# The weight pipeline of a two-layer hybrid trunk: low parts asked for three pieces ahead, later coefficients, a split eviction of u

## The chip, the cores and the metric

The kernel runs on one core of a Trainium2 chip. The core has a matrix engine (PE, with PEld for its weight loads), a vector engine (DVE), a scalar engine (ACT), GpSimd (POOL), a sync engine (SP) that here only starts DMAs, and 16 DMA engines. Each engine works off its own instructions in the order in which they were written and waits on semaphores for the others. The metric is the device time of one execution in microseconds (us); less is better.

## The reference, cut to what matters

Input x is 256 tokens of 2048 features in fp32. There are two layers; each is a mixer and a feed-forward block:

```python
h = rmsnorm(x);  z = h @ W_in            # z = [q | k | v | u | gate_attn | gate_ssm]
A = sliding_window_attention(q, k, v)     # 16 heads of 64, 4 kv heads, window 128, ALiBi, sinks
s_t = a * s_(t-1) + B u_t                 # 64 groups, 64 complex states each, over all positions
B = glu(gelu(Re(C s) + D u))
m = sigmoid(gate_attn) * (A @ W_ab) + sigmoid(gate_ssm) * (B @ W_sb)
x = x + m @ W_out
x = x + (silu(h2 @ W_gate) * (h2 @ W_up)) @ W_fo     # h2 = rmsnorm(x), inner width 5632
```

All of it is compared in fp32.

## The kernel before

**Pieces.** Activations are kept transposed, features on the partitions and 256 tokens along the free axis, each value as a high and a low part. All weights come as 881 pieces of 128 x 4 x 256 fp32 (512 KB, one DMA each from SP, line 91). ACT casts the high part of a piece, `whi` (L106), DVE subtracts it from the piece and so makes the low part, `wlo` (L121), and PE multiplies (L295): 8 matmuls of 128x512 with `whi` (against both parts of the activation), then 8 of 128x256 with `wlo`. (In the very first slab of layer 0 they go one by one, at L303.) The pools hold four raw pieces (`LOADS`), four `whi` and four `wlo` (`PARTS`).

**Lead.** `Weights.get(i)` stands ahead of the matmuls of piece i: it writes the instruction for the high part of piece i+3, for the low part of piece i+2, and the load of piece i+6. `low` itself begins with `self.high(upto, cuts)`, so a low part that is asked for brings its high part with it if that is not written yet.

**Ticks.** `Clock` orders everything else. After the matmuls of each piece `products` calls `ck.tick()`, which writes the jobs that are due: `later(n, f)` is a call n ticks on, `stages(n, gen)` runs a generator a `yield` at a time, one tick apart, `at(n, ...)` counts from the start of the layer. So each engine's queue is: the instructions of `get(i)`, the matmuls of piece i (PE only), the jobs of the tick, then `get(i+1)`.

**A layer.** Slabs of W_in go first: u (4 slabs of 4 pieces), k and v, q (4 slabs), then the gates of the attention branch (`ga`), W_ab in 8 slabs of 2 pieces, and the gates of the state-space branch (`gs`). After these come W_glu, W_sb, W_out and the feed-forward block. Into the ticks of these slabs are put:

- the state-space scan (L757 to L769): 127 steps, each of two multiplications (L766) and four additions (L769) on DVE, spread evenly from tick `s0 = v0 + 9` to tick 110. `states_in` (PE and ACT) fills the state `S` at the eight ticks from `v0`. After the last step PE computes `ys` (L963) from `S`.
- `attend(j)`, 8 times a layer: scores on PE and a maximum on DVE (L855); a tick later the exponentials on ACT (L862), the denominator and its reciprocal on DVE (L864, L865), and four scalings on ACT with that reciprocal (L869); two ticks later the transposes, then the product with v and the split of the result into `ya` (ACT L351, DVE L161).
- the evictions of the `gs` slabs: a copy (ACT L343), an addition and a multiplication by the norm (DVE L344, L943), and two sigmoids (ACT L363).
- in layer 0 alone, ahead of the scan, the coefficients of both layers' state spaces, some 600 short DVE instructions from tick 1 (`coefficients`, `prepare`, L1115 to L1118).

**The start.** The first norm has its squares on ACT (L404), their sums on GpSimd (L412), and a matmul `ms` with a matrix of ones (L417) at tick 5, which needs the sums. Lines 429 to 437 write the first pieces' high and low parts around them: low parts of pieces 0 to 2 ahead of the squares, the high part of piece 3 after two squares and that of piece 4 after six. `evict_u` (L716 to L731) scales a slab of u on DVE and, in the same job, copies it into the layout of the states, four copies on ACT and four on DVE.

Of the kernel before, what the change touches and what calls it, by code (L numbers as in the profile page):

```python
# [49 lines left out]
class Weights:  # L50
# [76 lines left out]
            self.n_low += 1  # L127

    def get(self, i):
        self.high(i + 3)  # L130
        self.low(i + 2)
        self.load(i + 2 + self.LOADS)
        return self.ready.pop(i)


class Clock:
# [6 lines left out]
    def later(self, n, fn, *args):  # L143
        self.jobs.setdefault(self.now + max(n, 1), []).append((fn, args))

    def stages(self, n, gen, step=1):


        def go():
            if next(gen, "end") != "end":  # L150
                self.later(step, go)

        if n > 0:
            self.later(n, go)
        else:
            go()
# [11 lines left out]
def build(ctx, tc, a, out):  # L168
# [18 lines left out]
    def p8(x, shape, dt=F32):  # L187
        return big.tile(shape, dt, name=nm(x), tag="p8", bufs=8)
# [11 lines left out]
    later, stages = ck.later, ck.stages  # L200


    W = Weights(nc, wp)
# [136 lines left out]
    def whole(ps, x="wh"):  # L340

        t = t2(x)
        s.copy(t, ps[:, :, T:])  # L343
        v.tensor_add(t, t, ps[:, :, :T])  # L344
        return t
# [79 lines left out]
    def x_in(i):  # L425
        return xs[i // 4][:, 2 * (i % 4) : 2 * (i % 4) + 2, :]
# [3 lines left out]
    for i in range(8):  # L430
        norm.feed(i, x_in(i))
        if i in lows:
            W.low(lows[i])
    for i in range(8):
        if i in (2, 6):
            W.high(3 + i // 4)
        norm.square(i, x_in(i))


# [3 lines left out]
    def vexp(dst, x, w):  # L443
        n, r, q = w
        v.tensor_scalar(dst, x, -103.9, 88.7, ALU.max, ALU.min)
        yield
        v.tensor_scalar(n, dst, math.log2(math.e), MAGIC, ALU.mult, ALU.add)
        yield
        v.tensor_scalar_sub(n, n, MAGIC)
        yield  # L450
        v.scalar_tensor_tensor(r, n, -0.693359375, dst, ALU.mult, ALU.add)
        yield
        v.scalar_tensor_tensor(r, n, 2.12194440e-4, r, ALU.mult, ALU.add)
        yield
        v.tensor_scalar_mul(q, r, 1.9875691500e-4)
        yield
        for c in (1.3981999507e-3, 8.3334519073e-3, 4.1665795894e-2, 1.6666665459e-1, 5.0000001201e-1):
            v.scalar_tensor_tensor(q, q, c, r, ALU.add, ALU.mult)
            yield
        v.scalar_tensor_tensor(q, q, 1.0, r, ALU.add, ALU.mult)  # L460
        yield
        v.tensor_scalar_add(dst, q, 1.0)
        yield

        half = r
        v.tensor_scalar(half, n, 0.5, MAGIC, ALU.mult, ALU.add)
        yield
        v.tensor_scalar_sub(half, half, MAGIC)
        yield
        v.tensor_sub(n, n, half)  # L470
        yield
        for m in (half, n):
            v.tensor_scalar(m, m, 127.0, 8388608.0, ALU.add, ALU.mult)
            yield
            v.tensor_copy(q.bitcast(I32), m)
            yield
            v.tensor_mul(dst, dst, q)
            yield
# [83 lines left out]
    def coefficients():  # L562
        v.tensor_reduce(pmask, ident.rearrange("p (q g h) -> p g q h", g=2, h=16), axis=AX.XY, op=ALU.add)
        v.tensor_scalar_mul(qg, qkg[:, :, 0], 0.125)
        ww = p8("cw", [P, 11, NC])
        w = [ww[:, i, :] for i in range(8)]
        dt, mag, th = (ww[:, i, :] for i in range(8, 11))
        yield from vexp(dt, ldt, w[:3])
        v.tensor_mul(mag, lam_r, dt)
        v.tensor_mul(th, lam_i, dt)  # L570
        chains = [vexp(mag, mag, w[:3]), vsincos(a_i, a_r, th, w[3:8])]
        while chains:
            chains = [c for c in chains if next(c, "end") != "end"]
            yield
        den, p, q, ar1, p2, q2 = w[:6]
        v.tensor_mul(a_r, a_r, mag)
        v.tensor_mul(a_i, a_i, mag)
        v.tensor_mul(den, lam_r, lam_r)
        v.tensor_scalar_sub(ar1, a_r, 1.0)
        v.tensor_mul(p2, lam_i, lam_i)  # L580
        yield
        v.tensor_mul(p, ar1, lam_r)
        v.tensor_mul(q, a_i, lam_i)
        v.tensor_add(den, den, p2)
        v.tensor_mul(p2, a_i, lam_r)
        v.tensor_mul(q2, ar1, lam_i)
        yield
        v.tensor_add(f_r, p, q)
        v.reciprocal(p, den)
        v.tensor_sub(f_i, p2, q2)  # L590
        yield
        v.tensor_mul(f_r, f_r, p)
        v.tensor_mul(f_i, f_i, p)

        v.tensor_mul(p, a_r, a_r)
        v.tensor_mul(q, a_i, a_i)
        v.tensor_mul(q2, a_r, a_i)
        yield
        v.tensor_sub(p, p, q)
        v.tensor_scalar_mul(n_ai, a_i, -1.0)  # L600
        v.tensor_scalar_mul(q2, q2, 2.0)
        for l in range(L):
            f = slice(32 * l, 32 * l + 32)
            yield
            v.tensor_copy(scan_c[:, l, 0, 0, :], p[:, f])
            v.tensor_copy(scan_c[:, l, 1, 1, :], p[:, f])
            v.tensor_copy(scan_c[:, l, 1, 0, :], q2[:, f])
            v.tensor_scalar_mul(scan_c[:, l, 0, 1, :], q2[:, f], -1.0)

    def sliced(gen, counts):  # L610

        counts = iter(counts)
        n = next(counts)
        for _ in gen:
            n -= 1
            while n <= 0:
                yield
                n = next(counts, 5)
# [86 lines left out]
    def layer(l, norm):  # L705
# [4 lines left out]
        def at(n, fn, *args):  # L710
            later(t0 + n - ck.now, fn, *args)
# [5 lines left out]
        def evict_u(i, ps, wide):  # L717
            x = whole(ps) if wide else ps[:, :, :T]
            v.tensor_mul(
                u[:, 2 * i : 2 * i + 2, :, :].rearrange("p s m c -> p s c m"),  # L720
                x.rearrange("p s (c m) -> p s c m", m=2),
                over(rms).rearrange("p s (c m) -> p s c m", m=2),
            )
            for j in range(4):
                for m in range(2):
                    o = 64 * (j % 2) + 32 * m
                    dst, src = ur[o : o + 32, 4 * i + j // 2 : 4 * i + 4 : 2, :], u[32 * j : 32 * j + 32, 2 * i : 2 * i + 2, m, :]
                    if m:
                        v.tensor_copy(dst, src)
                    else:  # L730
                        s.copy(dst, src)  # L731
# [19 lines left out]
        for i in range(4):  # L751
            wide = l > 0 or i > 0
            ps = slab((l, "in", 6 + i), norm.rhs, wide)
            later(1 if i else 3, evict_u, i, ps, wide)
        v0 = 17 if l else 30
        for n in range(8):
            at(v0 + n, states_in, n)  # L757

# [13 lines left out]
        def c_times_a():  # L772
            hold["cc"] = cw = p8("cc", [P, 4, 32, 16])
            for i, n in enumerate(("c_re", "c_im")):
                nc.sync.dma_start(cw[:, i], a[n][:, l])
            yield
            v.tensor_scalar_mul(cw[:, 1], cw[:, 1], -1.0)
            for i, signs in ((0, (a_r, a_i)), (1, (n_ai, a_r))):
                yield
                w = t2("ct", [P, 32, 16])  # L780
                v.tensor_mul(cw[:, 2 + i], cw[:, 0], per_pair(signs[0], l))
                v.tensor_mul(w, cw[:, 1], per_pair(signs[1], l))
                yield
                v.tensor_add(cw[:, 2 + i], cw[:, 2 + i], w)

        at(10 if l else 24, stages, 0, c_times_a())


        s0, s1 = v0 + 9, 110
# [31 lines left out]
        ps = slab((l, "in", 4), norm.rhs, True)  # L821
        stages(1, normed(kt, ps, qkg[:, l, 1:2]))
        ps = slab((l, "in", 5), norm.rhs, True)
        stages(1, values(ps))
        for i in range(4):
            ps = slab((l, "in", i), norm.rhs, True)
# [71 lines left out]
        for i in range(8):  # L898
            if i % 4 == 0:
                ga.append(p8("ga", [P, 8, T]))  # L900
            ps = slab((l, "in", 10 + i), norm.rhs, True)
# [16 lines left out]
        for i in range(8):  # L918
            ps = slab((l, "ab", i), lambda k: ya[k // 4][:, k % 4, :, :], True)
# [76 lines left out]
        for i in range(8):  # L996
            if i % 4 == 0:
                gs.append(p8("gs", [P, 8, T]))
            ps = slab((l, "in", 18 + i), norm.rhs, True)
# [14 lines left out]
        for i in range(4):  # L1014
            ps = slab((l, "glu", i), lambda k: yg[:, 0, k, :, :], True)
# [13 lines left out]
        for i in range(2, 8):  # L1029
            ps = slab((l, "sb", i), lambda k: yg[:, 1, k, :, :], True)  # L1030
# [13 lines left out]
        for i in range(8):  # L1044
            xo = t2("xo")
            nc.sync.dma_start(xo, src[:, 2 * i : 2 * i + 2, :])
            ps = slab((l, "o", i), lambda k: mg[:, k, :, :], True)
# [28 lines left out]
        for part, nf in enumerate(FPARTS):  # L1076
            hid = [p8("hid", [P, 4, 2, T], F32R) for _ in range(nf // 4)]
            for i in range(nf // 2):
                ps = slab((l, "fg", f0 // 2 + i), norm2.rhs, True)
                stages(3 if part == 0 and i == 0 else 1, gate(ps, i))  # L1080
                ps = slab((l, "fu", f0 // 2 + i), norm2.rhs, True)
# [14 lines left out]
            for i in range(8):  # L1096
# [3 lines left out]
                ps = slab((l, "fo", part, i), hrhs, True)  # L1100
# [11 lines left out]
            f0 += nf  # L1112
        return nxt

    stages(1, sliced(coefficients(), (5, 5, 5, 5, 4, 4, 4)))  # L1115
    first = prepare(0, v, 1)
    later(1, next, first)
    stages(15, first)  # L1118
    for l in range(L):
        norm = layer(l, norm)  # L1120
    ck.flush()
# [60 lines left out]
```

## Time and profile before

| what | us |
|---|---|
| median of three runs | 2632.5 (2630.88 to 2633.15) |
| the profiled execution | 2632.42 |
| its span, first to last instruction | 2630.5 |
| PE busy in the span | 2591.1 (99%) |
| DVE busy | 1932.4 (73%) |
| ACT busy | 1267.8 (48%) |
| GpSimd busy | 29.0 (1%) |

The profiled execution is within 0.1 us of the median, and 1.9 us of it lie outside the span. The shares are means over stages of different kinds: forty equal slices of the span show DVE at 90% or more in five of them and at 50 to 70% in most others, so each stage is to be read by itself.

### The profile page before, as it was taken

To read this page: it belongs to the slowest core of one execution; us is meant where nothing else is said; L and a number is where in the kernel's file an instruction comes from. 1 tells how busy PE (TensorE), PEld (TensorE's weight loads), DVE (VectorE), ACT (ScalarE), POOL (GpSimd) and SP (SyncE) were. 2 spreads that over 40 slices of the span, in tenths; PEclk is the share of its full clock that TensorE was granted. 3 is DMA by queue.
4 is the path that set the end of the run, shared out by engine and by line. 5 is a ranking of instruction groups with operands and counts; after the bars stand their busy time and mean duration, and the time that the engine had idled before them with its cause. 6 is when DMAs were issued, how large, how long until landed. Compare 5 with 4: busy or idle time off the path is not lost.

```text
span 2630.5 us, 40564 instructions
## 1 busy us (share of the span) xinstructions
PE 2591.1 (99%) x15716; PEld 2259.7 (86%) x15716; DVE 1932.4 (73%) x3648; ACT 1267.8 (48%) x1725; POOL 29.0 (1%) x34
## 2 busy tenths in 40 slices
PE   7999899999999999999999999999999999999999
PEld 6878788888888888888888788888888888888888
DVE  8889997866765666566677999887666656665664
ACT  5666545544443444334455675465544434443442
POOL 2000000000000000000000000000000000000000
PEclk9999999999999999999999999999999999999999
DMA  6544455666655565566664445556656556655655
GB/s 203 169 129 144 145 170 164 200 209 194 203 172 191 190 189 179 192 199 187 199 201 160 141 149 170 178 173 211 213 185 187 183 199 188 190 186 187 188 180 172
DMA packets 139825, 477.85 MB, mean 182 GB/s; under 512 B 14960, under 2 KB 25456, under 8 KB 139632
## 3 DMA queue, kind: packets, MB, share of 16 engines
q1 hardware_dynamic: 139488, 475.06, 56.4%
q8 instruction: 123, 2.02, 0.3%
q14 instruction: 70, 0.57, 0.1%
q10 hardware_dynamic: 144, 0.20, 0.0%
HBM read 471.01 MB, written 4.19 MB: 181 GB/s over the span
## 4 chain that ended last, share of the span: by engine, by line
PE 81%; DVE 14%; ACT 3%; issue 1%; DMA 0%; SPq 0%; ACTq 0%; DVEq 0%
PE acc L295 79%; DVE wlo L121 5%; DVE S L769 3%; DVE sc L766 2%; ACT whi L106 1%; DVE wh L344 1%; DVE scs L855 1%; PE v L746 1%; PE ys L963 1%; ACT scs L869 1%; DVE ga L896 0%; DVE ga L916 0%; DMA w<-in_w_in 0%; PE acc L323 0%; PE bt L672 0%
## 5 line engine op out<-in xcount | busy, mean ns | idle before, releaser
L106 ACT CAST whi<-w 128x1024 fp32r<-128x1024 f32 (+1 forms) x881 | 910.6, 1047 | 769.6 <-PE acc L295 606.4
L121 DVE TENSOR_TENSOR wlo<-w,whi 128x1024 fp32r<-128x1024 f32 (+1 forms) x881 | 1061.4, 1219 | 221.2 <-ACT whi L106 220.2
L295 PE MATMUL acc<-h,whi 128*128 128x512 f32 x4448 | 1128.6, 396 | 0.8 <-DVE wh L344 0.8
L295 PEld LDWEIGHTS acc<-h,whi 128*128 128x128 f32 x4448 | 802.3, 189 | 156.8 <-issue 9.4
L295 PEld LDWEIGHTS acc<-h,wlo 128*128 128x128 f32 x4448 | 606.1, 190 | 53.5 <-DVE wlo L121 10.9
L295 PE MATMUL acc<-h,wlo 128*128 128x256 f32 x4448 | 621.8, 283 | 5.3 <-DVE wlo L121 5.3
L295 PE MATMUL acc<-hid,whi 128*128 128x512 f32 x1384 | 346.6, 392 | 0.0
L295 PEld LDWEIGHTS acc<-hid,whi 128*128 128x128 f32 x1384 | 248.9, 189 | 44.5
L337 DVE TENSOR_REDUCE j<-acc 128x512 f32<-128x1024 f32 x88 | 107.8, 1225 | 134.4 <-PE acc L295 134.4
L295 PEld LDWEIGHTS acc<-hid,wlo 128*128 128x128 f32 x1384 | 188.8, 190 | 13.5
L295 PE MATMUL acc<-hid,wlo 128*128 128x256 f32 x1384 | 193.0, 282 | 0.0
L1102 DVE TENSOR_TENSOR xn<-xn,acc 128x512 f32<-128x512 f32 x47 | 32.3, 688 | 173.5 <-PE acc L295 173.5
L769 DVE TENSOR_TENSOR S<-S,sc 128x32 f32<-128x32 f32 x1016 | 153.5, 222 | 0.0
L295 PE MATMUL acc<-mg,whi 128*128 128x512 f32 x512 | 128.2, 392 | 0.0
L766 DVE TENSOR_TENSOR sc<-scan_c,S 128x64 f32<-128x64 f32 x508 | 115.6, 269 | 0.0
L295 PEld LDWEIGHTS acc<-mg,whi 128*128 128x128 f32 x512 | 92.1, 189 | 16.5
L295 PE MATMUL acc<-yg,whi 128*128 128x512 f32 x384 | 96.2, 392 | 0.0
L295 PEld LDWEIGHTS acc<-yg,whi 128*128 128x128 f32 x384 | 69.1, 189 | 12.3
L295 PE MATMUL acc<-ya,whi 128*128 128x512 f32 x256 | 68.5, 410 | 10.0 <-DVE ya L161 6.0
L295 PEld LDWEIGHTS acc<-mg,wlo 128*128 128x128 f32 x512 | 69.8, 190 | 5.0
L351 ACT CAST hid<-j 128x512 fp32r<-128x512 f32 x44 | 27.4, 623 | 96.9 <-DVE j L1072 96.9
L295 PE MATMUL acc<-mg,wlo 128*128 128x256 f32 x512 | 71.4, 282 | 0.0
(238 smaller groups left out, 1500.7 us busy)
## 6 DMA issues: line engine op xcount, KB each, us to landing
w<-in_w_fi SPq DMA_DIRECT2D x352, 512.0 KB, 4.3
w<-in_w_in SPq DMA_DIRECT2D x207, 512.0 KB, 3.7
w<-in_w_fo SPq DMA_DIRECT2D x176, 512.0 KB, 4.4
w<-in_w_out SPq DMA_DIRECT2D x64, 512.0 KB, 4.4
w<-in_w_ab SPq DMA_DIRECT2D x32, 512.0 KB, 3.5
w<-in_w_sb SPq DMA_DIRECT2D x32, 512.0 KB, 4.1
w<-in_w_glu SPq DMA_DIRECT2D x16, 512.0 KB, 3.8
x<-in_x SPq DMA_DIRECT2D x8, 256.0 KB, 5.8
```

The source lines that it names most:

```text
L106: self.nc.scalar.copy(part[0][:, f, :], w[:, f, :])
L121: self.nc.vector.tensor_sub(lo[:, f, :], w[:, f, :], hi[:, f, :].bitcast(F32))
L295: pe.matmul(o, w, r, start=start, stop=last and j == m - 1 and lo_part == 1, skip_group_check=True)
L337: v.tensor_reduce(t, ps.rearrange("p s (a t) -> p s t a", a=2), axis=AX.X, op=ALU.add)
L344: v.tensor_add(t, t, ps[:, :, :T])
L351: s.copy(hi, src)
L746: pe.matmul(pss[r][:, c0 : c0 + P], bt[ri][o : o + 64, 2 * q4 + i, :], ur[o : o + 64, 2 * q4 + i, :], start=True, stop=True)
L766: v.tensor_mul(pr, scan_c[:, l, :, :, f], S[:, :, f, c - 1].unsqueeze(1).to_broadcast([P, 2, 2, 16]))
L769: v.tensor_add(S[:, :, f, c], S[:, :, f, c], pr[:, :, r, :])
L855: v.tensor_tensor_reduce(scs[b][:, f, :], scs[b][:, f, :], pv[:, f, :], 1.0, sk[:, b : b + 1], ALU.add, ALU.max, accum_out=mx[:, b, n : n ...
L869: s.activation(z, z, AF.Copy, scale=rd[:, b, n : n + 1])
L1102: v.tensor_add(t, t, ps[:, :, :T])
```

## The change

The change has four parts. (1) `get(i)` now asks for the low part of piece i+3 (which brings the high part of i+3 with it, just ahead) and loads up to piece i+7; the low part of piece 3 is asked for ahead of the first squares, and no high part between them. (2) `evict_u` copies u a tick after it has scaled it. (3) `states_in` of layer 0 begins at tick 34 instead of 30, and with it the scan, whose last tick stays 110; the product `c_times_a` goes from tick 24 to 28. (4) The coefficients begin at tick 5 instead of 1, `prepare` at 19 instead of 15. The pools are as before. After the change the lines from L132 on are one lower, those from 435 on two lower, and those from 724 on one lower again.

```diff
     def get(self, i):
-        self.high(i + 3)
-        self.low(i + 2)
-        self.load(i + 2 + self.LOADS)
+        self.low(i + 3)
+        self.load(i + 3 + self.LOADS)
         return self.ready.pop(i)
...
         if i in lows:
             W.low(lows[i])
+    W.low(3)
     for i in range(8):
-        if i in (2, 6):
-            W.high(3 + i // 4)
         norm.square(i, x_in(i))
...
                 over(rms).rearrange("p s (c m) -> p s c m", m=2),
             )
+            yield
             for j in range(4):
...
-            later(1 if i else 3, evict_u, i, ps, wide)
-        v0 = 17 if l else 30
+            stages(1 if i else 3, evict_u(i, ps, wide))
+        v0 = 17 if l else 34
...
-        at(10 if l else 24, stages, 0, c_times_a())
+        at(10 if l else 28, stages, 0, c_times_a())
...
-    stages(1, sliced(coefficients(), (5, 5, 5, 5, 4, 4, 4)))
+    stages(5, sliced(coefficients(), (5, 5, 5, 5, 4, 4, 4)))
     first = prepare(0, v, 1)
     later(1, next, first)
-    stages(15, first)
+    stages(19, first)
```

What moves in the queues is seen at three places. The first is an `attend` in layer 0. ACT before: the exponentials and scalings of one `attend` (`scs`, `sm`), with the high parts of pieces 56 and 57 (`w_56`, `w_57`) on either side.

```order
L106 CAST whi_2330<-w_56_2186 128x1024
L862 ACTIVATE scs_2303,sm_2301<-scs_2303,sm_2301 128x128
...
L869 ACTIVATE scs_2303<-scs_2303,sm_2301 128x128
L869 ACTIVATE scs_2303<-scs_2303,sm_2301 128x256
L869 ACTIVATE scs_2306<-scs_2306,sm_2301 128x128
L869 ACTIVATE scs_2306<-scs_2306,sm_2301 128x256
L106 CAST whi_2380<-w_57_2224 128x1024
```

DVE before, at the same `attend`: the reciprocal that ACT's L869 needs, the low part of an earlier `ya`, and the next low part of weights, which is that of piece 56.

```order
L864 TENSOR_TENSOR sm_2301<-sm_2301 128x4
L865 RECIPROCAL sm_2301<-sm_2301 128x4
L161 TENSOR_TENSOR ya_1661<-y_2318,ya_1661 128x256
L121 TENSOR_TENSOR wlo_2331<-w_56_2186,whi_2330 128x1024
L766 TENSOR_TENSOR sc_2402<-scan_c,S_1271 128x64
```

ACT's rows stand in the same order after the change. DVE after, at the same place (lines one lower):

```order
L863 TENSOR_TENSOR sm_2256<-sm_2256 128x4
L864 RECIPROCAL sm_2256<-sm_2256 128x4
L160 TENSOR_TENSOR ya_1628<-y_2273,ya_1628 128x256
L121 TENSOR_TENSOR wlo_2336<-w_57_2141,whi_2335 128x1024
L765 TENSOR_TENSOR sc_2357<-scan_c,S_1380 128x64
```

What stands behind the reciprocal on DVE is now the low part of piece 57, whose high part stands on ACT behind the four scalings; before it was that of piece 56, whose high part stands ahead of the exponentials.

The second place is the eviction of a `gs` slab. DVE before, the multiplication by the norm and what follows it:

```order
L344 TENSOR_TENSOR gs_4112<-gs_4112,acc_3912 128x512
L943 TENSOR_TENSOR gs_4112<-gs_4112,rms_126 128x512
L121 TENSOR_TENSOR wlo_4071<-w_95_3959,whi_4070 128x1024
```

DVE after, and ACT after, with the two sigmoids (L362) that need that multiplication:

```order
L343 TENSOR_TENSOR gs_4099<-gs_4099,acc_3899 128x512
L942 TENSOR_TENSOR gs_4099<-gs_4099,rms_126 128x512
L121 TENSOR_TENSOR wlo_4106<-w_96_3946,whi_4105 128x1024
```

```order
L342 COPY gs_4099<-acc_3899 128x512
L362 ACTIVATE gs_3898<-gs_4099,params 128x256 x2
L106 CAST whi_4105<-w_96_3946 128x1024
```

The low part behind the multiplication is now that of piece 96, whose high part stands on ACT behind the sigmoids; before it was piece 95.

The third place is the start. DVE before, from the last parts of h (L400) on; L563 to L453 and L455 are the first coefficients:

```order
L400 SCALAR_TENSOR_TENSOR h_124<-x_78,params,h_124 128x256
L563 TENSOR_REDUCE pmask<-ident 128x2
L564 TENSOR_SCALAR qg<-params 128x2
L445 TENSOR_SCALAR cw_245<-params 128x64
...
L453 SCALAR_TENSOR_TENSOR cw_245<-cw_245 128x64
L121 TENSOR_TENSOR wlo_178<-w_3_93,whi_177 128x1024
L455 TENSOR_SCALAR cw_245<-cw_245 128x64
```

DVE after, from the same place on:

```order
L399 SCALAR_TENSOR_TENSOR h_124<-x_78,params,h_124 128x256
L121 TENSOR_TENSOR wlo_174<-w_3_93,whi_173 128x1024
L121 TENSOR_TENSOR wlo_251<-w_4_211,whi_250 128x1024
L121 TENSOR_TENSOR wlo_281<-w_5_213,whi_280 128x1024
L121 TENSOR_TENSOR wlo_311<-w_6_215,whi_310 128x1024
```

The low parts of pieces 3 to 6 now stand directly behind h, and the coefficients behind them.

## Rows read from the trace of the kernel before

**Rows 1.** The chain that ended last, shares of the span by engine.

```profile
PE 81%; DVE 14%; ACT 3%; issue 1%; DMA 0%; SPq 0%; ACTq 0%; DVEq 0%
```

**Rows 2.** Stretches: window, length, busy us (count) PE, PEld, DVE, ACT, POOL; clock, DMA, GB/s.

```profile
152.00:400.00 248.00, 233.81 (x1375) 195.02 (x1373) 242.85 (x987) 142.06 (x274) 3.63 (x2) 0.98 0.48 152
400.00:1400.00 1000.00, 1000.00 (x6090) 879.70 (x6084) 677.46 (x747) 457.65 (x543) 4.47 (x3) 1.00 0.59 191
1422.00:1694.00 272.00, 266.06 (x1581) 226.76 (x1580) 266.88 (x1011) 161.69 (x298) 3.63 (x2) 0.99 0.52 161
```

**Rows 3.** Timeline: start, duration (us), engine, instruction, [wait before it <-released by]; scan's end, layer 0.

```profile
399.32 3.57 PE L963 MATMUL ys<-S,cb 128*32 128x127 f32 x64 [2.06 <-DVE S L769]
```

**Rows 4.** Timeline, the same in layer 1.

```profile
1693.90 0.60 DVE L769 TENSOR_TENSOR S<-S,sc 128x32 f32<-128x32 f32 x4
1693.97 1.98 PE L963 MATMUL ys<-S,cb 128*32 128x127 f32 x64
```

**Rows 5.** Timeline, an `attend` of layer 0 on DVE and ACT.

```profile
199.81 0.18 DVE L865 RECIPROCAL sm<-sm 128x4 f32<-128x4 f32 x1
199.91 0.39 DVE L161 TENSOR_TENSOR ya<-y,ya 128x256 fp32r<-128x256 f32 x1
200.22 1.22 DVE L121 TENSOR_TENSOR wlo<-w,whi 128x1024 fp32r<-128x1024 f32 x1
200.09 1.50 ACT L869 ACTIVATE scs<-scs,sm 128x128 f32<-128x128 f32 x4 [2.64 <-DVE sm L865]
201.49 1.98 ACT L106 CAST whi<-w 128x1024 fp32r<-128x1024 f32 x2
```

**Rows 6.** Timeline, a low part that waits for its high part before the scan.

```profile
170.66 1.23 DVE L121 TENSOR_TENSOR wlo<-w,whi 128x1024 fp32r<-128x1024 f32 x1 [0.57 <-ACT whi L106]
```

**Rows 7.** Timeline, the eviction of a `gs` slab in layer 0, DVE and ACT.

```profile
351.34 0.69 DVE L943 TENSOR_TENSOR gs<-gs,rms 128x512 f32<-128x512 f32 x1
351.94 1.22 DVE L121 TENSOR_TENSOR wlo<-w,whi 128x1024 fp32r<-128x1024 f32 x1
352.07 0.91 ACT L363 ACTIVATE gs<-gs,params 128x256 f32<-128x256 f32 x2 [2.90 <-DVE gs L943]
352.88 2.93 ACT L106 CAST whi<-w 128x1024 fp32r<-128x1024 f32 x3
```

**Rows 8.** Timeline, the last `ya` of layer 0, DVE and ACT.

```profile
285.36 1.22 DVE L121 TENSOR_TENSOR wlo<-w,whi 128x1024 fp32r<-128x1024 f32 x1
285.44 1.04 ACT L106 CAST whi<-w 128x1024 fp32r<-128x1024 f32 x1 [0.74 <-PE acc L295]
```

**Rows 9.** Timeline, PE in the first 75 us.

```profile
24.81 0.58 PE L303 MATMUL acc<-h,wlo 128*128 128x256 f32 x1 [6.25 <-DVE wlo L121]
33.03 1.02 PE L417 MATMUL ms<-ssq,ones 128*128 128x256 f32 x4
53.71 1.21 PE L295 MATMUL acc<-h,wlo 128*128 128x256 f32 x8 [0.85 <-DVE wlo L121]
67.39 1.22 PE L295 MATMUL acc<-h,wlo 128*128 128x256 f32 x8 [2.25 <-DVE wlo L121]
68.44 3.58 PE L295 MATMUL acc<-h,whi 128*128 128x512 f32 x8
72.81 2.00 PE L295 MATMUL acc<-h,whi 128*128 128x512 f32 x8
```

**Rows 10.** Timeline, DVE and GpSimd at the start.

```profile
23.54 1.21 DVE L121 TENSOR_TENSOR wlo<-w,whi 128x1024 fp32r<-128x1024 f32 x1
16.69 10.56 POOL L412 TENSOR_TENSOR ssq<-ssq,sq 128x512 f32<-128x512 f32 x7 [12.87 <-ACT sq L404]
22.27 3.62 POOL L412 TENSOR_TENSOR ssq<-ssq,sq 128x512 f32<-128x512 f32 x2
```

**Rows 11.** Timeline, the first steps of the scan in layer 0 on DVE.

```profile
154.23 0.46 DVE L766 TENSOR_TENSOR sc<-scan_c,S 128x64 f32<-128x64 f32 x2
155.12 0.47 DVE L766 TENSOR_TENSOR sc<-scan_c,S 128x64 f32<-128x64 f32 x2
168.01 1.20 DVE L121 TENSOR_TENSOR wlo<-w,whi 128x1024 fp32r<-128x1024 f32 x1
```

## The prediction, made before the result was known

> **What bounds the kernel now.** I began with the chain that ended last: PE holds 81% of it and DVE 14% [rows 1]. Only the stages where DVE is on it can answer to a change of DVE's queue, so the second view is the busy time by stretch [rows 2]. From 400 to 1400 us PE is busy in all of 1000 us and DVE in 677: whatever DVE waits for there is covered by 323 us of its own idle time, and I cost the change at nothing there (the last stage is the same block again). The two stretches that hold the scans are different. In layer 0, 152 to 400 us, DVE is busy 242.85 of 248 us, and in layer 1, 1422 to 1694 us, 266.88 of 272. Both end where PE takes the finished state: in layer 0 PE stands 2.06 us waiting for the last scan additions [rows 3], in layer 1 `ys` begins 0.07 us after the last group of additions began [rows 4]. So from the scan's start to its end the time is DVE's work plus DVE's idle time, and there are only some 5 us of that in either. Each microsecond that the change makes DVE stand in these stretches is one of the total. The third view is therefore the timeline of DVE beside ACT, at each place where one waits for the other.
>
> **The change part by part.** *The low part a piece earlier.* Its work is the same: 881 casts and 881 subtractions. What moves is who stands behind whom. Before, the high part that a low part needs was written one `get` earlier; now both are written in the same `get`, so the low part can begin only when ACT has worked off everything up to it, and the matmuls no longer need it for three pieces. Where ACT's queue ahead of that cast itself waits for DVE, DVE stands for a round trip, and its scan steps, queued behind the low part, stand with it.
>
> At an `attend` this is so. DVE finishes the reciprocal at 199.99, ACT starts the four scalings at 200.09, and they take 1.50; the cast behind them starts at 201.49 and one takes 0.99 (two in 1.98), so it ends at 202.48 [rows 5]. DVE now starts its low part at 200.22, behind the low part of `ya`; it would start at 202.48: 2.3 us of standing. A row close to it: behind the first `attend` a low part waits to 170.66 for its high part, 0.57 us, although one scan step now stands ahead of it [rows 6]; the place behind the reciprocal, where it will stand, came at 168.01 [rows 11], 2.65 earlier. So I bound a trip by 0.57 and 2.65 and take the 2.3 of the row in the dense part. It applies to `attend` 0 to 6 (behind the seventh's reciprocal an eviction stands first); in layer 0 the first falls ahead of the later scan. That is 6 + 7 = 13 trips, 13 x 2.3 = 29.9.
>
> At a `gs` eviction the multiplication starts at 351.34, the two sigmoids take 0.91 from 352.07, and three casts start at 352.88, the first of them ending about 353.9 (2.93 for three). The low part now starts at 351.94 [rows 7], and would at 353.9: 2.0 us. Four such evictions lie before the last scan step of each layer: 8 x 2.0 = 16.0.
>
> At the last `ya` the low part at 285.36 would wait for the cast that runs from 285.44 to 286.48 [rows 8]: 1.1 us, in both layers 2.2.
>
> When PE comes to `ys` in layer 1 it will have waited, as in layer 0 now. There the same matmuls take 3.57 after the wait [rows 3] and 1.98 without one [rows 4]: +1.6.
>
> *Loads.* They go up to piece i+7 instead of i+6, each behind the low part that frees its buffer, as before; nothing else stands in SP's queue. DMA engines are busy 0.48 to 0.59 of a stretch [rows 2]: nothing. If a load came late, its cast would, by up to one piece.
>
> *The start.* The low part of piece 3 now stands directly behind h on DVE instead of behind the first coefficients. PE stood 6.25 us for it at 18.56 to 24.81 [rows 9], since DVE came to it at 23.54 [rows 10]. That goes; what is late next is the sum of squares. The seven additions on GpSimd run from 16.69 for 10.56 us; two of them, beside that low part, took 3.62, the other five 6.94, 1.39 each, so one meeting costs 0.84 to 2.23 minus 1.39 = 0.84 us [rows 10]. After the change ACT casts the high part of piece 3 ahead of the squares, so they begin one cast later (1.04, [rows 8]), and four low parts may meet them instead of one: 16.69 + 1.04 + 10.56 + 3 x 0.84 = 30.8, where PE, 6.25 us ahead, is at `ms` (33.03 now) at 26.8 or, at full clock, somewhat earlier. So it waits there again, and comes out 33.03 - 30.8 = 2.2 us ahead. The later waits of 0.85 and 2.25, and the 1.58 us that the next piece takes longer behind the latter (3.58 against 2.00, [rows 9]) go if coefficients that begin four ticks later no longer stand in the way, or come again in other places, since the same instructions are only moved. I bound PE's lead at the scan's start by -3 (all that was gained is lost at `ms`, and the waits come again) and +8 (6.25 + 0.85 + 2.25 + 1.58 = 10.9, less 3 for a shorter wait at `ms`) and take +2, near the `ms` row.
>
> The Trainium skill ("SBUF — State Buffer", section "Who interferes with whom") says that a vector instruction with two inputs in SBUF contends with a GpSimd instruction that reads SBUF, and that the loser waits for the whole instruction. The two slow additions agree; if the four low parts met no addition, the sums would end at 28.3 and the lead be 4.7, the forecast 2.7 lower.
>
> *The later scan.* In layer 0 the scan begins four ticks later with the same last tick. At 168.01, about where it will begin, seven steps lie behind it now, one each 0.89 us (154.23 to 155.12, [rows 11]): 6.2 us of DVE's work are pushed into the full stretch. Given back are one low part, which is by then done ahead (1.22, [rows 5]), and about as much again, my estimate of how much earlier DVE comes to that place without the steps: 6.2 - 2.4 = 3.8, less the lead of 2: +1.8.
>
> *The copies of u* come one tick later, ahead of the scan, and the first `states_in` that needs the last slab stands five ticks behind: nothing; if a copy were late, it would cost up to one piece (2.00 + 1.21 = 3.2, [rows 9]).
>
> The sum: 29.9 + 16.0 + 2.2 + 1.6 + 1.8 = 51.5. The profiled execution took 2632.4, the median of the runs is 2632.5: 2632.4 + 51.5 = **2683.9**, 2.0% slower.
>
> A sentence of the skill bears on the heart of it. The rows show DVE's low part starting as the next thing behind the reciprocal and `ya` [rows 5], with nothing overtaking. The Trainium skill ("TensorE: Matmul & The Clock Gate", the table at its head) gives ScalarE and VectorE strict first-in-first-out queues: by that nothing behind a waiting low part could fill the trip, and the trace agrees (DVE spends the 0.57 of [rows 6] idle, though it has more to do).
>
> **Rivals.** (1) *Faster.* The round trips cost nothing, because DVE comes to them late enough to find the cast done, and the start's waits go: the upper lead of 8, and the 2.06 of [rows 3], since a lead of 8 is more than the 3.8 of the later scan and lets DVE end before PE asks: 10, or **2622**. What decides is whether DVE finds the high part ready behind L865. Against it: the scalings can't begin before that reciprocal, however late DVE is, and stand ahead of the cast. (2) *No change.* The trips are hidden and the start's gain is eaten by `ms` and the denser scan: 2632 to **2634**. (3) *Half.* In layer 1 PE waits little (busy 266.06 of 272, [rows 2]), so its scan may have room that the rows don't show, and only layer 0 counts: 1.8 + 6 x 2.3 + 4 x 2.0 + 1.1 = 24.7, **2657**. Against it are the 0.07 us in rows 4. (4) *The clock too.* Each new wait of PE may be followed by a piece that takes 1.58 longer, as behind the wait of 2.25 [rows 9]. In layer 0 PE has 14 us of room for it, in layer 1, where PE and DVE are equally full, none: 11 trips x 1.58 = 17.4, **2701**.
>
> **How the numbers follow.** The forecast has 0.58, (1) 0.10, (2) 0.07, (3) 0.13, (4) 0.12. A measurement of this kernel tells some 0.2% (5 us) from no change. Faster is (1): 0.10; within it is (2): 0.07; slower are the rest: 0.83. The range leaves out (1) and (2), 0.17. It takes in (3) with 2 us below it and (4) with the upper bound of a trip (13 x 0.35 = 4.6) above it: 2655 to 2706. With trips of only 0.57 the time is 2683.9 - 13 x 1.73 = 2661, and the bounds of the lead move it by -6 and +5, all inside.
>
> **What would show it.** Right: DVE idle in the two scan stretches grows from 5 us to about 25 each, put down to `whi` of ACT on the low part behind each reciprocal and each `gs` multiplication, some 2 us each; PE waits for low parts in about as many places; the last scan addition of layer 0 ends some 25 us later, that of layer 1 some 50. The wait of 6.25 is gone and `ms` starts at 30 to 31. Wrong: low parts behind the reciprocal without a wait; a scan that ends in layer 1 only 25 us later (3); or PE's granted clock falling well below 0.98 in these stretches (4).

## The result and the profile after

The changed kernel takes 2736.97 us (four runs, 2736.5 to 2739.12) against 2632.57 before: 1.0399 times as long, 95% interval 1.0381 to 1.0417, or 104 us more. Slower was forecast, and by the mechanism that was named, but the 51 us forecast are half of it, and the time lies outside the range (2655 to 2706).

The page's chain of the changed kernel, by engine, answers to [rows 1]; under it stands the group of the low parts in the same page (busy us, mean ns, idle before them, what released most of it).

```profile
PE 76%; DVE 16%; ACT 4%; issue 3%; POOL 0%; DMA 0%; SPq 0%; ACTq 0%; DVEq 0%; POOLq 0%
L121 DVE TENSOR_TENSOR wlo<-w,whi 128x1024 fp32r<-128x1024 f32 (+1 forms) x881 | 1072.3, 1225 | 648.8 <-ACT whi L106 648.4
```

Before, the same 881 low parts had 221.2 us of idle time ahead of them. So DVE now stands some 430 us more for high parts, over the whole program. Only a quarter of that has become time. Where it did is read from one event on PE at a time, in both kernels: the start of the first matmul of a stage.

| from ... to (PE) | before, us | after, us | more | forecast |
|---|---|---|---|---|
| start ... first W_ab, layer 0 | 0 to 275.91 | 0 to 292.33 | +16.4 | 15.6 |
| ... first `gs` slab | 332.10 | 351.37 | +2.9 | 1.1 |
| ... end of the wait for the state, at `ys` | 399.32 | 427.97 | +9.4 | 8.0 |
| ... first W_glu | 438.50 | 472.28 | +5.1 | 0 |
| ... first W_out | 505.54 | 555.74 | +16.4 | 0 |
| ... first W_ab, layer 1 | 1580.77 | 1652.40 | +21.4 | 16.1 |
| ... first `gs` slab | 1631.87 | 1705.29 | +1.8 | 1.1 |
| ... `ys` | 1693.97 | 1774.75 | +7.4 | 8.0 |
| ... first W_glu | 1731.50 | 1818.20 | +5.9 | 1.6 |
| ... first W_out | 1798.54 | 1900.84 | +15.6 | 0 |
| ... end | 2630.5 | 2734.5 | +1.7 | 0 |

(The 21.4 of the sixth line are 3.6 from W_out to the second layer's norm and 17.8 behind it, of which 3.1 lie ahead of the first `attend`.) Down to `ys` of either layer the forecast nearly holds: 24.7 us more were forecast for layer 0 and 28.7 measured, for layer 1's mixer 25.2 and 27.0. Most of what it lacks lies behind the scan, from `ys` to the first matmul of W_out: 21.5 us in each layer, where the forecast had nothing in the first and 1.6 in the second.

### The profile page after: what moved, and what is told of

It reads as the page before. It is cut to its first block, busy times and chain, and to the rows that moved or that the text cites. A ratio compares the mean times of both kernels' runs of the same rounds, so it can differ in the third digit from the quotient of the medians.

```text
span 2734.5 us, 40715 instructions
## 1 busy us (share of the span) xinstructions
PE 2620.3 (96%) x15716; PEld 2276.9 (83%) x15716; DVE 1938.3 (71%) x3648; ACT 1258.1 (46%) x1725; POOL 31.7 (1%) x34
## 4 chain that ended last, share of the span: by engine, by line
PE 76%; DVE 16%; ACT 4%; issue 3%; POOL 0%; DMA 0%; SPq 0%; ACTq 0%; DVEq 0%; POOLq 0%
PE acc L294 73%; DVE wlo L121 6%; DVE S L768 3%; ACT whi L106 2%; DVE sc L765 2%; ACT scs L868 1%; DVE scs L854 1%; PE ys L962 1%; PE v L745 1%; DVE wh L343 1%; POOL ssq L411 0%; DVE mg L160 0%; PE acc L322 0%; DVE sb L1023 0%; DVE sb L1024 0%
## 5 line engine op out<-in xcount | busy, mean ns | idle before, releaser
L121 DVE TENSOR_TENSOR wlo<-w,whi 128x1024 fp32r<-128x1024 f32 (+1 forms) x881 | 1072.3, 1225 | 648.8 <-ACT whi L106 648.4
L106 ACT CAST whi<-w 128x1024 fp32r<-128x1024 f32 (+1 forms) x881 | 900.8, 1045 | 651.2 <-PE acc L294 504.9
L294 PE MATMUL acc<-yg,whi 128*128 128x512 f32 x384 | 103.5, 414 | 25.1 <-DVE glu L343 12.3
L294 PEld LDWEIGHTS acc<-yg,whi 128*128 128x128 f32 x384 | 72.2, 197 | 41.5 <-DVE glu L343 13.2
L362 ACT ACTIVATE sg<-j 128x512 f32<-128x512 f32 x44 | 27.9, 633 | 139.1 <-DVE j L1060 139.1
```

Of the source, the lines that this page charges most:

```text
L106: self.nc.scalar.copy(part[0][:, f, :], w[:, f, :])
L121: self.nc.vector.tensor_sub(lo[:, f, :], w[:, f, :], hi[:, f, :].bitcast(F32))
L294: pe.matmul(o, w, r, start=start, stop=last and j == m - 1 and lo_part == 1, skip_group_check=True)
L362: s.activation(o, i, AF.Sigmoid, **kw)
```

## The trips, as they were foretold

The timeline of the changed kernel at an `attend` in layer 0, DVE, ACT and PE; columns as in [rows 3], and it answers to [rows 5].

```profile
204.37 0.18 DVE L864 RECIPROCAL sm<-sm 128x4 f32<-128x4 f32 x1
204.46 0.39 DVE L160 TENSOR_TENSOR ya<-y,ya 128x256 fp32r<-128x256 f32 x1
204.64 1.49 ACT L868 ACTIVATE scs<-scs,sm 128x128 f32<-128x128 f32 x4 [2.69 <-DVE sm L864]
205.10 1.53 PE L875 MATMUL pt<-ident,scs 128*128 128x128 f32 x6 [3.02 <-ACT scs L868]
206.04 1.98 ACT L106 CAST whi<-w 128x1024 fp32r<-128x1024 f32 x2
...
207.10 1.23 DVE L121 TENSOR_TENSOR wlo<-w,whi 128x1024 fp32r<-128x1024 f32 x1 [2.25 <-ACT whi L106]
```

Read it from the reciprocal: ACT has stood 2.69 us for it, scales, casts; then DVE, which has stood 2.25 for that cast, goes on. Before, the low part stood directly behind `ya` with no wait at all. This wait occurs seven times in each layer: the first is 2.56 long, the others 2.25 (2.3 was forecast). The same at a `gs` eviction, which answers to [rows 7]:

```profile
370.59 0.69 DVE L942 TENSOR_TENSOR gs<-gs,rms 128x512 f32<-128x512 f32 x1
...
371.32 0.91 ACT L362 ACTIVATE gs<-gs,params 128x256 f32<-128x256 f32 x2 [4.65 <-DVE gs L942]
372.13 1.98 ACT L106 CAST whi<-w 128x1024 fp32r<-128x1024 f32 x2
...
373.19 1.23 DVE L121 TENSOR_TENSOR wlo<-w,whi 128x1024 fp32r<-128x1024 f32 x1 [1.91 <-ACT whi L106]
```

It is 1.91 in seven of the eight places before the last scan steps and 1.92 in the eighth (2.0 was forecast). In the windows that answer to the scan stretches of [rows 2], DVE's idle time (length less busy time) has grown from 5 us to 27 and 31 (columns as there):

```profile
168.00:428.00 260.00, 223.15 (x1278) 186.92 (x1277) 233.16 (x960) 132.71 (x255) 3.63 (x2) 0.96 0.44 135
1475.00:1775.00 300.00, 275.67 (x1589) 231.82 (x1591) 269.39 (x1012) 160.99 (x298) 3.63 (x2) 0.98 0.49 148
```

## The stretch that the prediction had averaged away

The windows from the first W_glu matmul to the first W_out matmul, layer 0, first of the kernel before and then of the changed one, same columns.

```profile
438.50:505.54 67.04, 67.04 (x387) 59.01 (x385) 56.27 (x67) 40.64 (x58) 0.00 (x0) 1.00 0.64 201
```

```profile
472.28:555.74 83.46, 72.75 (x385) 62.50 (x385) 56.25 (x67) 40.26 (x57) 0.00 (x0) 0.94 0.50 156
```

Before, PE is busy in all of it, but DVE has 56.27 of 67.04 us of work: its cover, the idle time that could take up new waits, is 10.8 us. What fills it after the change is DVE's longest entry among the waits of the changed kernel's window (engine and line, waited for: us in total, times, longest us):

```profile
DVE wlo L121 <- ACT whi L106: 26.4, 15, 2.0
```

56.25 + 26.4 = 82.65 of 83.46 us: DVE has become the bound, and 26.4 of standing less 10.8 of cover is 15.6, near the 16.4 that the stage grew. (Before, 0.5 us of such waits stood in the window.) How it reaches PE is seen in the timeline at a slab of W_sb:

```profile
529.85 0.69 DVE L1024 TENSOR_TENSOR sb<-sb,ga 128x512 f32<-128x512 f32 x1
530.58 0.62 ACT L350 CAST mg<-sb 128x512 fp32r<-128x512 f32 x1 [3.83 <-DVE sb L1024]
...
531.10 1.99 ACT L106 CAST whi<-w 128x1024 fp32r<-128x1024 f32 x2
...
532.18 1.23 DVE L121 TENSOR_TENSOR wlo<-w,whi 128x1024 fp32r<-128x1024 f32 x1 [1.64 <-ACT whi L106]
533.00 0.58 ACT L342 COPY sb<-acc 128x512 f32<-128x512 f32 x1
533.32 0.68 DVE L160 TENSOR_TENSOR mg<-sb,mg 128x512 fp32r<-128x512 f32 x1
...
533.92 1.22 DVE L121 TENSOR_TENSOR wlo<-w,whi 128x1024 fp32r<-128x1024 f32 x1
535.06 0.68 DVE L343 TENSOR_TENSOR sb<-sb,acc 128x512 f32<-128x512 f32 x1
...
535.79 2.11 PE L294 MATMUL acc<-yg,whi 128*128 128x512 f32 x8 [0.79 <-DVE sb L343]
```

It is the pattern of `attend` with other names: DVE's last step of an eviction, a cast on ACT that needs it, ACT's cast of the weights behind that, and DVE's low part behind both. What PE waits for is not the low part but the accumulator: there are two, and DVE empties one of them 0.79 us too late. From `ys` to W_glu, where 5.1 and 5.9 us were lost, the low parts wait in the same way, by the trace 1.0 to 1.9 us six times in layer 0, 9.5 us together. Idle time does not explain that loss: DVE had 11.7 us of it there before (27.48 busy of 39.18). But DVE also waits 8.2 us for PE's `ys` in that stage, and at its end PE itself waits for a high part:

```profile
472.28 2.74 PE L294 MATMUL acc<-yg,whi 128*128 128x512 f32 x8 [3.26 <-ACT whi L106]
```

So this stage loses time as a chain of ACT, DVE and PE, and not by DVE's being full; no run took it apart.

## The experiments

Each ran beside the kernel before on the same chip; ratios are to that one, and the excess of a run is its median less the median of the kernel before beside it.

**The change of `get` alone**, on the kernel before:

```diff
-        self.high(i + 3)
-        self.low(i + 2)
-        self.load(i + 2 + self.LOADS)
+        self.low(i + 3)
+        self.load(i + 3 + self.LOADS)
```

> The kernel before with the change of get alone: low part of piece i+3 and load of i+7, everything else (start, coefficients, evict_u, v0) as before. Theory (round trips: the low part stands on DVE right behind the high part of the same get, and ACT's queue ahead of that one waits for DVE): all of the loss is here. 13 trips of 2.25 and 8 of 1.91 in the scans, and some 16 us in each layer's glu and sb slabs: +95 to +115 us, 2728 to 2748. Rival (the later scan and the moved coefficients make the loss, since they crowd the same DVE): under +60, below 2693.

2743.82 us, ratio 1.0429 (1.0412 to 1.0446): +113. All of the loss is in this part, and more than all: the rest of the change, with a lead of three, is worth some 8 us (113 against 104; the intervals of the two ratios just overlap). PE's waits in this run say where: in the first 100 us, with coefficients from tick 1, PE stands 4.22 for u and twice 2.2 for a high part, which the changed kernel does not show.

```profile
45.30 3.75 PE L294 MATMUL acc<-h,whi 128*128 128x512 f32 x8 [4.22 <-DVE u L718]
...
72.54 2.11 PE L294 MATMUL acc<-h,whi 128*128 128x512 f32 x8 [2.22 <-ACT whi L106]
...
86.18 2.11 PE L294 MATMUL acc<-h,whi 128*128 128x512 f32 x8 [2.20 <-ACT whi L106]
```

**The rest alone**: the changed kernel with the three lines of `get` as before.

> The changed kernel with the get of before (high part of i+3, low part of i+2, load of i+6); the early low part of piece 3, the later coefficients and scan and the split of evict_u stay. Round-trip theory: no loss is left; the start gives 0 to 6 us back and the denser scan of layer 0 takes up to 4: 2626 to 2636. Rival (crowding): +40 us or more, above 2670.

2633.77, ratio 1.0007 (0.9998 to 1.0016), +2.5 or nothing. PE comes to `ms` 3.2 us earlier (29.83 against 33.03), is still 2.4 ahead at the scores of the first `attend`, about where the scan begins, and 1.5 behind at `ys` (400.81 against 399.32): the denser scan costs 3.9. The crowding of DVE by the later scan is not the cause of the loss.

**The high part four pieces ahead**, with a fifth buffer for it, so that the low part, still three ahead, again stands a `get` behind it:

```diff
-        self.low(i + 3)
+        self.high(i + 4)
+        self.low(i + 3)
...
-                ... tag=n, bufs=self.PARTS) for n in ("whi", "wlo"))
+                ... tag=n, bufs=self.PARTS + (n == "whi")) for n in ("whi", "wlo"))
```

> The changed kernel with the high part asked for four pieces ahead and a fifth buffer for it, so that the low part of i+3 again stands one get behind its high part. To make room the temporaries t2 have 6 buffers instead of 7 and sc 2 instead of 4. Round-trip theory: the waits of 2.25 and 1.91 behind reciprocal and gs multiplication vanish, 2625 to 2645. Rival (it is the lead of three itself, with four buffers of low parts, which lets a low part begin only when PE is done with piece i-1): the loss stays, above 2690. If the smaller temporary pools hurt, a wait for their buffers shows on ACT or DVE.

2638.63, ratio 1.0027 (1.0017 to 1.0038). Its excess of 7.4 us stands against 104.4: 97 us are gone with the lead of three left in place. The timeline of DVE at the same `attend` shows the low part behind `ya` with no wait, as in [rows 5]:

```profile
199.98 0.18 DVE L865 RECIPROCAL sm<-sm 128x4 f32<-128x4 f32 x1
200.08 0.39 DVE L161 TENSOR_TENSOR ya<-y,ya 128x256 fp32r<-128x256 f32 x1
200.39 1.22 DVE L121 TENSOR_TENSOR wlo<-w,whi 128x1024 fp32r<-128x1024 f32 x1
```

So neither the lead nor the four buffers of low parts cost the time, but that both halves of a piece are asked for in one place. Why it stays above the kernel before, and 5 us above the rest alone, the theory does not say. One suspect was tested:

**The smaller temporaries** that made room for that buffer, in the kernel before (`t2` with 6 buffers instead of 7, `sc` with 2 instead of 4).

> The kernel before with 6 buffers of t2 and 2 of sc, as in the run with the high part four ahead, which was 5 us slower than the rest alone. If the smaller temporaries made those 5 us: 2634 to 2638. If the lead of three made them: 2630 to 2633.

2630.93, ratio 0.9999 (0.9989 to 1.0008): not these. By PE's events the loss against the rest alone is there at the end of layer 0's scan (the wait at `ys` ends at 404.15 against 400.81) and hardly grows later; its cause stays open.

**The lead of three everywhere but in W_glu and W_sb** (`d` is 2 for their 24 pieces in each layer, 3 for the others):

```diff
+        d = 2 if i in self.close else 3
+        self.high(i + 3)
+        self.low(i + d)
+        self.load(i + d + self.LOADS)
```

> The changed kernel, but with the get of before for the pieces of W_glu and W_sb alone (24 of each layer's pieces). Theory: the step missed in the prediction is that DVE is nearly full there too, 56 of 67 us, and the round trips behind the evictions of these slabs cost 16.4 and 15.6 us from the first glu to the first W_out matmul; those go and nothing else: 2700 to 2709. Rival (those slabs only inherit a lateness that the scan left, and would lose it elsewhere): 2725 to 2737.

2706.56, ratio 1.0286 (1.0271 to 1.0301): its excess is 75.3 us, 29 less than the changed kernel's. From the first W_glu to the first W_out matmul, layer 0, it takes 68.7 us (473.87 to 542.57) where the changed kernel takes 83.5. These slabs do not pass on a lateness of the scan; they make their own.

**The lead of three in W_glu and W_sb alone**, on the kernel before, with the same lines turned round:

> The kernel before, with the changed get (low part of i+3, load of i+7) for the pieces of W_glu and W_sb alone, 24 of each layer. Nothing is late when these slabs begin. Theory: the trips fill DVE there by themselves: the 30 us that leaving these pieces out gave back, 2658 to 2665. Rival (the slabs only pass on the lateness of a slower scan): below 2640.

2660.27, ratio 1.0107 (1.009 to 1.0124): +29, from the other side. Here nothing was late when the slabs began, and each layer's stretch grows by 14.4 us. The waits of the window from 438.50 to 520 us (the lines of this kernel stand one lower, L122 for L121):

```profile
DVE wlo L122 <- ACT whi L107: 24.6, 15, 1.9
```

**The lead of three in W_out and the feed-forward block alone**, on the kernel before:

> The kernel before, with the changed get for the pieces of W_out and of the feed-forward block alone (three quarters of all pieces). DVE is busy two thirds of the time there. The prediction's step that the change costs nothing there: 2630 to 2634. The milestones of the changed kernel say otherwise by a little (1.2 us in each W_out, 2.4 at the first layer's second norm): 2635 to 2638.

2632.18, ratio 1.0002 (0.9992 to 1.0011): nothing, over 592 of the 880 pieces (two thirds; the expectation has it too high, and the 881 subtractions count the first piece, which is cut in two, twice). So the 5 us that the table shows from W_out on do not come from the trips of those stages alone; their cause stays open. What becomes of the trips is shown by DVE's longest waits from 594.9 to 1343 us, first in the kernel before, then in this run:

```profile
DVE wlo L121 <- ACT whi L106: 93.9, 89, 3.5
DVE xn L1102 <- PE acc L295: 82.3, 24, 4.2
DVE j L337 <- PE acc L295: 66.3, 43, 4.2
```

```profile
DVE wlo L122 <- ACT whi L107: 218.7, 154, 3.4
DVE xn L1108 <- PE acc L297: 23.9, 18, 1.4
DVE j L339 <- PE acc L297: 4.0, 3, 1.4
```

and the two windows, in the same order (columns as in [rows 2]):

```profile
594.90:1343.00 748.10, 748.10 (x4416) 658.70 (x4414) 496.34 (x520) 321.73 (x353) 4.47 (x3) 1.00 0.59 191
```

```profile
594.90:1343.00 748.10, 747.91 (x4417) 658.55 (x4416) 495.00 (x517) 316.96 (x353) 3.20 (x3) 1.00 0.61 191
```

Some 125 us of waits for high parts have come in, and some 121 us of waits for PE's accumulators have gone: DVE, which stood idle for 252 us here before, now stands idle for 253. It waits for ACT where it waited for PE, and PE does not notice.

**The scalings of `attend` a tick later**, in the changed kernel, so that ACT's cast behind the reciprocal waits for nothing of DVE:

```diff
             v.reciprocal(rd, den)
+            yield
             for b in range(2):
...
-            yield
             yield
```

> The changed kernel, with the four scalings of each attend on ACT a tick later (the reciprocal yields before them, and one tick is waited behind them instead of two). The low part behind the reciprocal then stands behind a high part that waits for nothing of DVE. Round-trip theory: the 13 to 14 waits of 2.25 go, and PE's waits for the scalings (3.02, 2.13, 3.00 ...) with them: 2737 - 31 = 2706, 2698 to 2714; the waits of 1.91 at gs and those in glu and sb stay. Rival (any low part in the same get as its high part costs, wherever ACT's other work stands): above 2725.

2703.64, ratio 1.0275 (1.0258 to 1.0292). Its excess over the kernel before is 72.2 us where the changed kernel has 104.4: 32 us for some 14 trips of 2.25. The timeline shows the reciprocal followed by a low part that does not wait:

```profile
201.93 0.18 DVE L864 RECIPROCAL sm<-sm 128x4 f32<-128x4 f32 x1
202.03 0.39 DVE L160 TENSOR_TENSOR ya<-y,ya 128x256 fp32r<-128x256 f32 x1
202.34 1.22 DVE L121 TENSOR_TENSOR wlo<-w,whi 128x1024 fp32r<-128x1024 f32 x1
```

**All of these a tick later**: the sigmoids of `gs` and the casts of `mg` (slabs 0 to 6) and of `yg` (W_glu slabs 0 to 2) as well.

> The same, and also the sigmoids of a gs eviction, the cast of mg in an sb eviction (slabs 0 to 6) and the cast of yg in a glu eviction (slabs 0 to 2) a tick later than the DVE instruction that they need. Round-trip theory: 2737 - 31 (attend) - 16 (gs) - 27 (of the 32 in glu and sb; the last slab of each keeps its trip) = 2663, 2650 to 2675. Rival (the trips only move to the next place): above 2695.

2657.07, ratio 1.0097 (1.0082 to 1.0112). Of the excess of 104.4, 78.8 are gone with `get` as changed. By PE's events the 25.6 that are left are 5 us in the W_glu and W_sb of each layer, 6 between the second layer's norm and its first W_ab, 6 by the end of layer 0's scan, and some smaller ones. Trips that were not moved are one part of that: in the W_glu and W_sb of layer 0 nine low parts still wait, 9.6 us together. Another part this run makes itself: there PE stands 2.9 us for low parts of `yg`, whose casts now come a tick later, a wait that the changed kernel does not have.

**The early low part of piece 3 alone**, on the kernel before:

```diff
+    W.low(3)
     for i in range(8):
-        if i in (2, 6):
-            W.high(3 + i // 4)
         norm.square(i, x_in(i))
```

> The kernel before with the early low part of piece 3 alone (asked for ahead of the squares, no high part between them); lead, coefficients, scan and evict_u as before. If the start's gain of 2 to 3 us at ms is real and is lost in the kernel with the rest alone only to the later scan: 2627 to 2630. If the coefficients from tick 1 take it back (they now stand behind more low parts): 2631 to 2634.

2631.46, ratio 1.0 (0.999 to 1.0009). The gain at `ms` is 1.2 us and is used up by the first `attend`. No version was found that beats the kernel before.

## Why the prediction was right and wrong

**What bounds the kernel: wrong in one step.** The two scan stretches were read rightly. The step that failed is the sentence on 400 to 1400 us: "DVE in 677: whatever DVE waits for there is covered by 323 us of its own idle time". A window of 1000 us was read as one stage. In it lie W_glu and W_sb, where DVE's cover is 10.8 us against 26.4 of trips, and the feed-forward block, where DVE is idle for 252 us and the trips only take the place of waits for PE. The first costs 29 us over both layers, by two runs from opposite sides; the second costs nothing, by a third. The same sentence covers the stage from `ys` to W_glu, which lost 5.1 and 5.9. Together these two stages lost 43 us where 1.6 were forecast: 41 of the 53 us by which the forecast fell short. A window of the kernel before from the first W_glu matmul to the first W_out matmul, as it stands above, would have shown how little cover there is.

**The trips of the scans: right in place, number and size but for one kind.** 13 by 2.3 and 8 by 2.0 were forecast; the trace shows 2.25 and 1.91, and two first ones of 2.56, of which that of layer 0 lies ahead of the scan. Taking the first kind away gave 32 us where 29.9 was forecast. The third kind, 1.1 at the last `ya` of each layer, did not come: from the last `attend`'s trip to the first `gs` eviction no low part waits for its high part in either layer. The stretch from W_ab to `gs` grew all the same, by 2.9 and 1.8, but by as much as DVE had more work in it (58.76 us against 55.91, 52.62 against 50.82), so that this term comes near is luck.

**The start: right in the mechanism, wrong in what is left of it at the scan.** `ms` was to start at 30.8, and not at the 26.8 that PE could have managed. PE's row and GpSimd's show it, and answer to [rows 9, 10]:

```profile
30.65 2.07 PE L416 MATMUL ms<-ssq,ones 128*128 128x256 f32 x4 [6.11 <-POOL ssq L411]
...
17.45 13.15 POOL L411 TENSOR_TENSOR ssq<-ssq,sq 128x512 f32<-128x512 f32 x7 [13.64 <-ACT sq L403]
...
21.45 8.02 DVE L121 TENSOR_TENSOR wlo<-w,whi 128x1024 fp32r<-128x1024 f32 x4 [3.59 <-ACT whi L106]
```

A wait of 6.25 for a low part has become one of 6.11 for the sums, and the four matmuls of `ms` behind it take 2.07 instead of 1.02, at a granted clock of 0.50 (the level of 1.2 GHz) instead of 1.00 (2.4 GHz). Four low parts meet the sums: they take 8.02 together, and the seven additions 13.15 instead of 10.56. Taken one by one, three of the low parts took 2.28 to 2.32 and four of the additions 2.12 to 2.16, one of each here:

```profile
24.99 2.28 DVE L121 TENSOR_TENSOR wlo<-w,whi 128x1024 fp32r<-128x1024 f32 x1
24.06 2.13 POOL L411 TENSOR_TENSOR ssq<-ssq,sq 128x512 f32<-128x512 f32 x1
```

Alone the one takes 1.22 and the other 1.27. Together one of each is done every 2.2 us, little less than the 2.49 of one after the other, and both sides pay. (In the row that the prediction read, 3.62 for two additions, only one of the two was slow, 2.27 after 1.27; a meeting costs 0.85 to 1.0 us, where 0.84 was put down.) The Trainium skill ("SBUF — State Buffer", section "Who interferes with whom") says that a DVE instruction with two inputs in SBUF contends with a GpSimd instruction that reads SBUF, and that the port pair they share is an exclusive lock; the trace agrees.

The lead of 2.4 us at `ms` (33.03 against 30.65) is gone when the scan begins, where +2 was forecast. The first scores of an `attend` on PE, in the kernel before, in the rest alone and in the changed kernel:

```profile
159.15 0.93 PE L850 MATMUL sc<-kv,q 64*128 64x128 f32 x8
```

```profile
156.72 0.82 PE L850 MATMUL sc<-kv,q 64*128 64x128 f32 x8
```

```profile
160.00 0.82 PE L849 MATMUL sc<-kv,q 64*128 64x128 f32 x8
```

With the rest alone PE is 2.4 ahead, and the denser scan then costs 3.9, where 3.8 was put down. In the changed kernel PE is 0.85 behind: the term of 1.8 is too small by 2.9, a part of the 4.0 by which layer 0 exceeds its forecast.

**The rivals.** Faster (1) and no change (2) fell with the timeline: the trips are there. Half (3) fell as well: the second layer's scan loses as much as the first. The clock (4) can't be seen as a cost of its own: removing some 32 us of trips at the `attend`s gave back 32, so a microsecond of standing costs about one. The granted clock did fall with the waits, in the two scan stretches from 0.98 and 0.99 to 0.96 and 0.98, over the span from 0.994 to 0.986, and rose again where the trips were taken away; no run holds the one fixed and moves the other.

## What to carry to other kernels

Two halves of one job on two engines that each work in order are to be asked for in different places, a slot apart: asked for together, the second half puts its engine behind everything that the first engine has queued, and if that in turn waits for the second engine, the trip is paid in full. A longer lead for both halves together does not help against this; a longer lead for the first half alone does (2638.63 us), and so does a tick's delay of the instructions that close the loop (2657.07).

And cover is counted per stage: 125 us of waits added to an engine that is busy in 66% of a stage took the place of its waits for PE and cost nothing, and 26 us of the same waits at 84% of a stage cost 14 to 16 us a layer, though PE was 100% busy in both. Idle time is cover only where nothing else depends on when it falls: from `ys` to W_glu DVE had enough of it, and the stage lost 5 us. Cut the windows where the work changes, not where the page's busy share looks flat.

## What the runs showed of the hardware that was not expected

Low parts on DVE and additions on GpSimd, running at the same time, lengthened each other: from 1.22 to some 2.3 us and from 1.27 to some 2.1 us each. Elsewhere nothing of the hardware was other than the rows of before had shown.
